# Four small edits to a TensorE-bound hybrid attention block: earlier mean squares, earlier activation sums, a tied order of the first splits, and another buffer ring for one tanh

## The chip, the cores and the metric

The kernel runs on one core of a Trainium2 chip. The metric is the device time of one execution in microseconds (us). Five engines work side by side, each through its own queue in order: TensorE (PE in the profile, with its weight loads as PEld), VectorE (DVE), ScalarE (ACT), GpSimd (POOL) and SyncE (SP), which only issues transfers here. ScalarE and GpSimd issue transfers too.

## The reference

One decoder block on x of 512 rows by 1024 columns, float32. Two attention branches of 8 heads of 64 read one normalised input:

```
h = rms_norm(x, norm_g)
proj = h @ w_in          # fq fk fv fz | mq mk mv mz | ga gb | fl
q, k = rms_norm per head (fq, fk); log_f = log_sigmoid(fl + b_f)
y_fox  = softmax(q k^T / 8 + cumsum(log_f) differences, causal) v * silu(fz)
q, k = partial_rope(rms_norm per head (mq, mk))
y_moba = block-sparse causal attention(q, k, mv) * silu(mz)
merged = sigmoid(ga + b0) * (y_fox @ w_fox) + sigmoid(gb + b1) * (y_moba @ w_moba)
out = x + merged @ w_out
```

With 512 rows and MoBA blocks of 256 all earlier blocks are selected, so that the second branch is plain causal attention in what it computes.

## The kernel before, in words

**Products in three parts.** Every product runs on operands that are split into a high part (rounded to the type that TensorE multiplies) and a low part (the rest): high × high, high × low and low × high are summed in PSUM. A split is one ScalarE copy for the high part and one VectorE subtraction for the low part. So each weight chunk that comes in (`wr`) becomes `wh` and `wl`, and each activation becomes a pair such as `Zh`/`Zl` or `Gh`/`Gl`.

**The start.** `first_loads` fetches the transposed x in 8 blocks (`XT`, tiles `xt`) and the first weight chunk in four pieces, by turns, on SyncE's queue. `first_split` (lines 148 to 160) splits the pieces of that chunk and, in the order of its argument `between`, the blocks of x (`split_x`, lines 120 to 126): `Zh`, `Zl`. For the first two pieces VectorE makes the high part too (line 155). `first_qk` multiplies the two first column groups, `fqa` and `fka`, from these unnormalised x (lines 382 to 384), four PSUM banks each, block after block of x; the factor of the row norm comes in later.

**The row norm.** `x_stats` (lines 221 to 232) loads x once more, not transposed, in 8 tiles, squares each on ScalarE with a running sum, and takes the power −1/2 on GpSimd: r. `norm_row` lays r out as a row with four TensorE transposes (bank `p_rbc`, line 240) and a ScalarE copy, `rbc`. `normalise` (lines 243 to 247) then multiplies the x blocks with it and splits them into `Gh` and `Gl`, which all later projections read; the first is `fva`.

**Attention.** Four groups of four heads (fox a, fox b, moba a, moba b) run one after another. In each, `Tr` transposes q and k, `Aa` makes logits in the two banks of "lg" (lines 555 and 556), subtracts the maximum on VectorE (`negm`, line 558) and takes exp on ScalarE (line 560), and `Bb` transposes the probabilities and multiplies with v (bank `pv`), after which ScalarE copies one half out (`ysh`, line 635) and VectorE adds the other. Between these steps the function `inter` puts units of other projections ("fill") by turns: in the first group 16 of them (`fqb`, `fkb`, `fvb`, `mqa`, four each), in the last `mzb` and the products with `w_fox` (`wf0` to `wf2`, banks `pf`). `unit_z` (lines 413 to 426) computes z·(1 + tanh(z/2)), twice the silu, straight from a PSUM bank of the ring "pj" (2 banks): tanh on ScalarE into a tile `sg`, then a VectorE operation into `zs` (line 425), which frees the bank. The factor 1/2 is put into the row sums of the softmax.

**Activation sums.** `make_sums(k)` (lines 257 to 277), for k from 0 to 3, makes four sums and differences of normalised x blocks on VectorE (line 265), splits them, and stores them to DRAM through ScalarE's queue (line 275). The "gates" stage reads them back for the `ga` and `gb` products, which run as a seven-product Strassen scheme.

**Who sets the order.** The program text only gives a priority: a planner goes through it with estimated times and writes each engine's queue, taking of what it holds ready the piece that stands first in the text. `tc.issue_after(ins)` ties the pieces of its block behind `ins` on that engine. Tiles come from rings by tag: "u" with 4 tiles of 128 × 512, "y" with 15, and in PSUM "pj" 2, "tp" 3, "lg" 2, "pv" 1. A tile can be had only when an earlier one of its ring has been released.

Of the kernel before, what the change touches and what calls it, by code (L numbers as in the profile page):

```python
# [7 lines left out]
F32 = mybir.dt.float32  # L8
F32R = mybir.dt.float32r
AF = mybir.ActivationFunctionType  # L10
OP = mybir.AluOpType
# [5 lines left out]
NT = S // P  # L17
KT = D // P
HD = 64
CW = 256  # L20
# [9 lines left out]
def fox_moba_kernel(ctx: ExitStack, tc, xT, x, w_in, w_fl, w_fox, w_moba, w_out, cst, rope, out):  # L30


    nc = tc.nc
    V, A, G, T = nc.vector, nc.scalar, nc.gpsimd, nc.tensor
# [14 lines left out]
    def t2(tag, bufs, name, shape=(P, 512), dt=F32):  # L49
        pool = stage["pool"] if tag in ("qs", "pt", "pc", "ys") else sb  # L50
        return pool.tile(list(shape), dt, name=name, tag=tag, bufs=bufs)
# [39 lines left out]
    def col(c, n=1):  # L91
        return cs[:, c:c + n]
# [13 lines left out]
    for i in range(WARM):  # L106
# [6 lines left out]
    G.memset(mask, 0.0)  # L113
    G.affine_select(mask[:, 384:512], mask[:, 384:512], pattern=[[-1, P]], compare_op=OP.is_ge,
                    fill=NEG, base=0, channel_multiplier=1)

    Gh = con.tile([P, KT, S], F32R, name="Gh")
    Gl = con.tile([P, KT, S], F32R, name="Gl")
# [2 lines left out]
    def split_x(*ks):  # L121
        for k in ks:
            xt = XT[k]
            zh, zl = Z[k] = [stage["pool"].tile([P, S], F32R, name=f"Z{hl}{k}") for hl in "hl"]
            A.activation(zh, xt, AF.Copy, scale=col(C_NG + k))
            V.scalar_tensor_tensor(zl, xt, col(C_NG + k), zh.bitcast(F32), op0=OP.mult, op1=OP.subtract)


    chunks = {}
# [18 lines left out]
    def first_split(hf, between):  # L148
        raw = RAW[hf]
        hi = sb.tile([P, 4, 264], F32R, name=f"wh_fqa{hf}", tag="wh", bufs=4)  # L150
        lo = sb.tile([P, 4, 264], F32R, name=f"wl_fqa{hf}", tag="wl", bufs=4)
        for q, xs in enumerate(between):
            k = slice(2 * q, 2 * q + 2) if hf else slice(max(q, 2 * q - 2), max(q + 1, 2 * q))
            if hf == 0 and q < 2:
                V.tensor_copy(hi[:, k, :CW], raw[:, k])
            else:
                A.activation(hi[:, k, :CW], raw[:, k], AF.Copy)
            V.tensor_tensor(out=lo[:, k, :CW], in0=raw[:, k], in1=hi[:, k, :CW].bitcast(F32), op=OP.subtract)
            split_x(*xs)
        chunks.setdefault("fqa", []).append((hi, lo))  # L160

# [59 lines left out]
    def x_stats():  # L221
        G.memset(mh, -0.5)
        for t in range(NT):
            for hf in range(2):
                xt = t2("y", 15, f"x{t}{hf}")
                nc.sync.dma_start(out=xt, in_=x[t * P:(t + 1) * P, hf * 512:(hf + 1) * 512])
                j = t2("u", 4, "junk")
                A.activation(j, xt, AF.Square, accum_out=ms2[:, t, hf:hf + 1])
        V.tensor_add(mm, ms2[:, :, 0], ms2[:, :, 1])
        V.tensor_scalar(mm, mm, 1.0 / D, EPS, op0=OP.mult, op1=OP.add)  # L230
        V.tensor_scalar(e2, mm, EPS, None, op0=OP.mult)
        G.tensor_tensor(out=r, in0=mm, in1=mh[:, :NT], op=OP.pow)
# [4 lines left out]
    def norm_row():  # L237
        p = pst("lg", 2, "p_rbc")
        for t in range(NT):
            T.transpose(p[:, t * P:(t + 1) * P], r[:, t:t + 1].to_broadcast([P, P]), ident)  # L240
        A.activation(rbc, p, AF.Copy)
# [132 lines left out]
    def first_qk(name, tags):  # L374
        banks = [pst(tg, n, f"{name}_{i}") for i, (tg, n) in enumerate(tags)]
        n = 264 if name == "fka" else CW
        for kk in range(KT):
            hi, lo = chunks[name][kk // 4]
            k = kk % 4
            for t in range(NT):  # L380
                st = slice(t * P, (t + 1) * P)
                T.matmul(banks[t][:, :n], Z[kk][0][:, st], hi[:, k, :n], start=(kk == 0), stop=False)
                T.matmul(banks[t][:, :n], Z[kk][0][:, st], lo[:, k, :n], start=False, stop=False)
                T.matmul(banks[t][:, :n], Z[kk][1][:, st], hi[:, k, :n], start=False, stop=(kk == KT - 1))
        return banks
# [27 lines left out]
    def unit_z(name, c):  # L413
        def go():
            p = (tp if name == "fzb" else pj)(f"pz_{name}{c}")
            tr_mm(p, name, c)
            z = t2("y", 15, f"zs_{name}{c}")
            s = t2("u", 4, "sg")
            if name[0] == "f":
                V.tensor_tensor(out=z, in0=p, in1=rbc, op=OP.mult)  # L420
                A.activation(s, z, AF.Tanh, scale=0.5)
                V.scalar_tensor_tensor(z, s, 1.0, z, op0=OP.add, op1=OP.mult)
            else:
                A.activation(s, p, AF.Tanh, scale=0.5)
                V.scalar_tensor_tensor(z, s, 1.0, p, op0=OP.add, op1=OP.mult)  # L425
            ZS[name[0], 2 * (name[2] == "b") + c] = z
        return go
# [586 lines left out]
                res.append(go)  # L1014
        return res

    def last_on(engine):
        return next(i for i in reversed(nc.cur_bb.bb.instructions) if i.engine == engine)

    def inter(a, b):  # L1020
        n, m = len(a), len(b)
        ia = ib = 0
# [9 lines left out]
        for u in filler(names):  # L1032
            u()

    first_split(0, ((0,), (1, 2), (3, 4)))
    first_split(1, ((5, 6), (7,)))
    nc.sync.dma_start(out=wfl, in_=w_fl)
    load_fl("fka", COLS["fka"], 0)
    load_fl("fka", COLS["fka"], 1)
    b1 = first_qk("fqa", (("pj", 2), ("pj", 2), ("lg", 2), ("lg", 2)))  # L1040
    b2 = first_qk("fka", (("tp", 3), ("tp", 3), ("tp", 3), ("pv", 1)))
    x_stats()
    for t in range(NT):
        evac_qk(b1[t], "fqa", t)
    for t in range(NT):
        evac_qk(b2[t], "fka", t)
    forget_exp()
    norm_row()
    pump(0)
    fz = filler(["fza", "fzb"])  # L1050
    for k, u in enumerate(fz):
# [14 lines left out]
    for n in range(4):  # L1066
        nxt = []

        def following(n=n, nxt=nxt):
            br, half, cq, ck = plan[n + 1][:4]  # L1070
            if n == 1:
                moba_begin()
            nxt.extend(attn_group(br, half, col(cq), col(ck)))
            nxt[0][0]()
        fill = filler(plan[n][4])
        if n == 0:
            for k in range(4):
                store = []

                at = 3 * k + 5  # L1080

                def with_sums(u=fill[at], k=k, store=store):
                    u()
                    with tc.issue_after(last_on(mybir.EngineType.DVE)):
                        store.append(make_sums(k))

                def with_store(u=fill[at + 1], store=store):
                    u()
                    store[0]()
                fill[at], fill[at + 1] = with_sums, with_store  # L1090
        inter(body + ([following] if n < 3 else []) + tail, fill)
        if n < 3:
            at = 2
            body, tail = nxt[1][:at] + gate + nxt[1][at:], nxt[2]
            gate = nxt[3]
# [10 lines left out]
    groups["WO"]()  # L1106
    prep, product, evac, sub, result = (groups[k] for k in ("prep", "product", "evac", "sub", "out"))

    def behind():
        return tc.issue_after(last_on(mybir.EngineType.DVE))  # L1110
    m1, m3 = filler(["wm1"]), filler(["wm3"])
    if True:
        m1[0]()
# [111 lines left out]
```

## Time and profile before

| | |
|---|---|
| median of 3 runs | 427.01 us (426.59 to 427.05) |
| the profiled execution's own time | 426.79 us |
| its span | 424.8 us |
| TensorE busy | 418.6 us, 99% |
| VectorE busy | 326.7 us, 77% |
| ScalarE busy | 269.3 us, 63% |
| GpSimd busy | 100.7 us, 24% |
| mean granted TensorE clock | 0.999 |

The span counts from the first to the last instruction of the program; some 2 us lie around it. In a row of a timeline stand the start and the length in us, engine, line, operation, out<-in by the program's names, the shape, and in brackets the idle time of the engine before it with what ended it. Rows of one tile give lengths in ns as least/median/most. A busy TensorE is not a TensorE at its peak, since matmuls overlap: there the distance from start to start is what counts.

### The profile page before, as it was taken

Reading aid. Unit: us, or ns where it says so; the run is one execution under the profiler, and the core shown is the slowest. Engines: PE = TensorE matmul, PEld = TensorE weight load, DVE = VectorE, ACT = ScalarE, POOL = GpSimd, SP = SyncE. Lnnn points to the kernel's source line nnn. Section 1 sums busy time; section 2 is a strip of 40 time slices with the busy share of each in tenths; the row PEclk is TensorE's granted clock in tenths of the full one; section 3 lists DMA queues with packets and bytes.
Section 4 is the critical chain, followed back from the end, with each engine's and each line's share of the span. In section 5 each row is a group of like instructions: output and inputs, shape, how many; then the busy total and the mean of one; then the engine's idle time right before and its main releaser. Section 6 shows DMA issues by size and latency. Waiting matters only on the chain.

```text
span 424.8 us, 7715 instructions
## 1 busy us (share of the span) xinstructions
PE 418.6 (99%) x2913; PEld 388.9 (92%) x2913; DVE 326.7 (77%) x570; ACT 269.3 (63%) x515; POOL 100.7 (24%) x120
## 2 busy tenths in 40 slices
PE   8999999999999999999999999999999999999996
PEld 7998899999999998899998878899999989988885
DVE  4669976769969878578576697767979598689893
ACT  4986426866857977567656687665756535686450
POOL 1049200225133950016650103140000000022330
PEclk9999999999999999999999999999999999999999
DMA  7981235225485423203124131663052603696484
GB/s 241 392 304 67 84 115 154 77 90 198 154 227 173 114 100 125 92 33 125 32 94 116 63 95 44 224 226 127 19 182 64 234 2 117 208 252 118 99 145 154
DMA packets 25621, 58.21 MB, mean 137 GB/s; under 512 B 3064, under 2 KB 7856, under 8 KB 25584
## 3 DMA queue, kind: packets, MB, share of 16 engines
q1 hardware_dynamic: 13392, 38.11, 26.6%
q10 hardware_dynamic: 8800, 11.21, 8.7%
q0 software_dynamic: 3392, 8.39, 8.6%
q8 instruction: 23, 0.38, 0.4%
q14 instruction: 14, 0.11, 0.1%
HBM read 48.11 MB, written 6.32 MB: 128 GB/s over the span
## 4 chain that ended last, share of the span: by engine, by line
PE 65%; DVE 1%; ACT 1%; issue 0%
PE pb_GB L753 3%; PE pb_GA L753 3%; PE pb_GA L750 3%; PE pb_GB L750 3%; PE pb_GB L752 3%; PE pb_GA L752 3%; PE po L941 3%; PE po L940 3%; PE po L939 3%; PE pf L679 2%; PE pv L611 2%; PE pm L681 2%; PE pf L681 2%; PE pf L680 2%; PE pv L610 2%; PE pm L680 2%
## 5 line engine op out<-in xcount | busy, mean ns | idle before, releaser
L560 ACT ACTIVATE p<-p,negm 128x128 f32<-128x128 f32 (+1 forms) x64 | 35.7, 559 | 20.8 <-DVE negm L558 18.4
L334 POOL TENSOR_TENSOR ff<-ss,mh 128x8 f32<-128x8 f32 x16 | 27.2, 1702 | 79.0 <-DVE ss L332 78.7
L558 DVE CUSTOM_DVE_ANT_0 p<-lg,mask 128x128 f32<-128x128 f32 (+1 forms) x64 | 30.5, 486 | 13.3 <-PE lg L556 13.1
L888 POOL DMA_DIRECT2D wr_o<-in_w_out_dram x4 | 4.9, 1295 | 95.4 <-ACT wr_o L887 95.4
L555 PE MATMUL lg<-KH,QS 128*128 128x128 f32 (+1 forms) x64 | 20.6, 333 | 0.2 <-DVE negm L558 0.2
L134 ACT ACTIVATE wh_GB<-wr_gb 128x1024 fp32r<-128x1024 f32 x14 | 14.6, 1059 | 9.5 <-PE pm L680 3.5
L136 DVE TENSOR_TENSOR wl_GA<-wr_ga,wh_GA 128x1024 fp32r<-128x1024 f32 x14 | 16.9, 1224 | 4.7 <-ACT wh_GA L134 3.9
L901 ACT ACTIVATE wh_o<-wr_o 128x1024 fp32r<-128x1024 f32 x14 | 14.8, 1057 | 8.3 <-PE pb_GB L752 2.8
L134 ACT ACTIVATE wh_GA<-wr_ga 128x1024 fp32r<-128x1024 f32 x14 | 14.6, 1059 | 8.3 <-issue 3.0
L902 DVE TENSOR_TENSOR wl_o<-wr_o,wh_o 128x1024 fp32r<-128x1024 f32 x14 | 17.0, 1222 | 3.7 <-ACT wh_o L901 3.4
L636 DVE TENSOR_TENSOR ypair<-pv,ysh 64x512 f32<-64x512 f32 x16 | 11.0, 688 | 11.2 <-ACT ysh L635 10.9
L136 DVE TENSOR_TENSOR wl_GB<-wr_gb,wh_GB 128x1024 fp32r<-128x1024 f32 x14 | 16.9, 1223 | 3.5 <-ACT wh_GB L134 3.5
L607 DVE TENSOR_TENSOR ptl<-p_a,pth 128x512 fp32r<-128x512 f32 x16 | 11.0, 686 | 6.8 <-ACT pth L606 6.7
L635 ACT ACTIVATE ysh<-pv 64x512 f32<-64x512 f32 x16 | 9.5, 593 | 7.8 <-POOL qn_mqa L336 2.5
L750 PE MATMUL pb_GA<-Gh,wh_GA 128*128 128x256 f32 x48 | 13.6, 282 | 0.0
L752 PE MATMUL pb_GA<-Gl,wh_GA 128*128 128x256 f32 x48 | 13.5, 281 | 0.0
L679 PE MATMUL pf<-yhf,wh_wf 128*128 128x512 f32 x32 | 12.8, 400 | 0.7 <-DVE zs_mzb L425 0.7
L753 PE MATMUL pb_GA<-Gh,wl_GA 128*128 128x256 f32 x48 | 13.5, 281 | 0.0
L753 PE MATMUL pb_GB<-Gh,wl_GB 128*128 128x256 f32 x48 | 13.5, 281 | 0.0
L752 PE MATMUL pb_GB<-Gl,wh_GB 128*128 128x256 f32 x48 | 13.4, 281 | 0.0
L750 PE MATMUL pb_GB<-Gh,wh_GB 128*128 128x256 f32 x48 | 13.3, 281 | 0.0
L529 DVE SCALAR_TENSOR_TENSOR QS<-p_qT,cs,QS 64x512 fp32r<-64x512 f32 x16 | 12.0, 750 | 1.6 <-ACT QS L528 1.1
(459 smaller groups left out, 1795.4 us busy)
## 6 DMA issues: line engine op xcount, KB each, us to landing
wr_ga<-in_w_in_dram SPq DMA_DIRECT2D x8, 512.0 KB
wr_gb<-in_w_in_dram SPq DMA_DIRECT2D x8, 512.0 KB
wr_o<-in_w_out_dram SPq DMA_DIRECT2D x8, 512.0 KB
xt<-in_xT_dram SPq DMA_DIRECT2D x8, 256.0 KB
x<-in_x_dram SPq DMA_DIRECT2D x8, 256.0 KB
KH<-KH ACTq DMA_DIRECT2D x16, 128.0 KB
s_dramh<-sum_sh ACTq DMA_DIRECT2D x8, 256.0 KB
s_draml<-sum_sl ACTq DMA_DIRECT2D x8, 256.0 KB
```

Source lines behind the costliest of these rows:

```text
L134: A.activation(hi[:, :, 0:n], src, AF.Copy)
L136: eng.tensor_tensor(out=lo[:, q, 0:n], in0=src[:, q], in1=hi[:, q, 0:n].bitcast(F32), op=OP.subtract)
L334: G.tensor_tensor(out=f2, in0=ss.rearrange("p t h -> p (t h)"), in1=mh, op=OP.pow)
L555: T.matmul(lg[:, :n], qs[:, qt], kh[:, :n], start=True, stop=False)
L558: V.tensor_tensor_reduce(pt, lg[:, :n], mask[:, 512 - n:512], -0.125, 3.0e38, op0=OP.add, op1=OP.min, accum_out=mkn[:, hh, i:i + 1])
L560: A.activation(pt, pt, AF.Exp, bias=mkn[:, hh, i:i + 1], scale=-1.0, accum_out=rs[:, hh, i:i + 1])
L679: T.matmul(p, hi[:, k, cc], yh, start=(k == 0), stop=False)
L680: T.matmul(p, hi[:, k, cc], yl, start=False, stop=False)
L750: T.matmul(o, hi[:, k, cc], lh, start=(n < 3 and c == 0 and k == 0), stop=False, skip_group_check=True)
L752: T.matmul(o, hi[:, k, cc], ll, start=False, stop=False, skip_group_check=True)
L753: T.matmul(o, lo[:, k, cc], lh, start=False, stop=(k == 3), skip_group_check=True)
L902: V.tensor_tensor(out=wide(lo), in0=wide(R[key, c]), in1=wide(hi).bitcast(F32), op=OP.subtract)
```

## The change

- Mean squares: the two tiles of the last quarter of x come from the ring "u" instead of "y"; ScalarE writes the squares over x itself instead of into a tile `junk`; and in the text the statistics, the evacuation of `fqa` and `norm_row` stand ahead of the products of `fka`.
- Activation sums: packet k is attached to fill unit 3k instead of 3k + 5, its stores to the unit after it.
- First splits: all their VectorE instructions are tied behind the last VectorE instruction of the text, so that VectorE takes them in the order of the text; and block 4 of x moves from the first half's last step to the second half's first one, with blocks 5, 6 and 7 following.
- The tanh of `mzb`: its tile `sg` comes from the ring "y" instead of "u".

The helpers `last_on` and `behind` move up in the file; what they do is unchanged.

```diff
+    def last_on(engine):
+        return next(i for i in reversed(nc.cur_bb.bb.instructions) if i.engine == engine)
+
+    def behind(engine=mybir.EngineType.DVE):
+        return tc.issue_after(last_on(engine))
...
             A.activation(zh, xt, AF.Copy, scale=col(C_NG + k))
-            V.scalar_tensor_tensor(zl, xt, col(C_NG + k), zh.bitcast(F32), op0=OP.mult, op1=OP.subtract)
+            with behind():
+                V.scalar_tensor_tensor(zl, xt, col(C_NG + k), zh.bitcast(F32), op0=OP.mult, op1=OP.subtract)
...
             if hf == 0 and q < 2:
-                V.tensor_copy(hi[:, k, :CW], raw[:, k])
+                with behind():
+                    V.tensor_copy(hi[:, k, :CW], raw[:, k])
             else:
                 A.activation(hi[:, k, :CW], raw[:, k], AF.Copy)
-            V.tensor_tensor(out=lo[:, k, :CW], in0=raw[:, k], in1=hi[:, k, :CW].bitcast(F32), op=OP.subtract)
+            with behind():
+                V.tensor_tensor(out=lo[:, k, :CW], in0=raw[:, k], in1=hi[:, k, :CW].bitcast(F32), op=OP.subtract)
             split_x(*xs)
...
-                xt = t2("y", 15, f"x{t}{hf}")
+                xt = t2("u", 4, f"x{t}{hf}") if t == NT - 1 else t2("y", 15, f"x{t}{hf}")
                 nc.sync.dma_start(out=xt, in_=x[t * P:(t + 1) * P, hf * 512:(hf + 1) * 512])
-                j = t2("u", 4, "junk")
-                A.activation(j, xt, AF.Square, accum_out=ms2[:, t, hf:hf + 1])
+                A.activation(xt, xt, AF.Square, accum_out=ms2[:, t, hf:hf + 1])
...
-            s = t2("u", 4, "sg")
+            s = t2("y", 15, "sg") if name == "mzb" else t2("u", 4, "sg")
...
-    first_split(0, ((0,), (1, 2), (3, 4)))
-    first_split(1, ((5, 6), (7,)))
+    first_split(0, ((0,), (1, 2), (3,)))
+    first_split(1, ((4, 5), (6, 7)))
...
     b1 = first_qk("fqa", (("pj", 2), ("pj", 2), ("lg", 2), ("lg", 2)))
-    b2 = first_qk("fka", (("tp", 3), ("tp", 3), ("tp", 3), ("pv", 1)))
     x_stats()
     for t in range(NT):
         evac_qk(b1[t], "fqa", t)
+    norm_row()
+    b2 = first_qk("fka", (("tp", 3), ("tp", 3), ("tp", 3), ("pv", 1)))
     for t in range(NT):
         evac_qk(b2[t], "fka", t)
     forget_exp()
-    norm_row()
...
-                at = 3 * k + 5
+                at = 3 * k
```

More of the change, by code (lines that the diff above doesn't have):

```diff
@@ L1015, in filler @@
         return res
-    def last_on(engine):
-        return next(i for i in reversed(nc.cur_bb.bb.instructions) if i.engine == engine)
     def inter(a, b):
@@ L1107, in fox_moba_kernel @@
     prep, product, evac, sub, result = (groups[k] for k in ("prep", "product", "evac", "sub", "out"))
-    def behind():
-        return tc.issue_after(last_on(mybir.EngineType.DVE))
     m1, m3 = filler(["wm1"]), filler(["wm3"])
```

## The prediction

> **What bounds the kernel now.** I read the engine totals of the page first, then TensorE's list of waits, then the timelines around each place where TensorE stood still, and last the load of VectorE by stretch.
>
> ```profile
> PE 418.6 (99%) x2913; PEld 388.9 (92%) x2913; DVE 326.7 (77%) x570; ACT 269.3 (63%) x515; POOL 100.7 (24%) x120
> ```
>
> TensorE (PE) is busy for 99% of the span of 424.8 us. The diff neither adds nor removes a matmul, so it can only win back time in which TensorE stood still, or add such time.
>
> ```profile
> PE pf L679 <- DVE zs_mzb L425: 0.7, 1, 0.7
> PE lg L555 <- DVE negm L558: 0.2, 1, 0.2
> ```
> ```profile
> 421.30:424.90 3.60, 0.00 (x0) 0.00 (x0) 0.42 (x1) 0.00 (x0) 0.00 (x0) 0.85 0.26 88
> ```
>
> After the start, the list of waits names just two: 0.7 us before the first product with `w_fox` and 0.2 us before a block of logits. The last row (busy time by engine from 421.30 on) is the tail, where TensorE has finished; the diff does not touch it. What can be gained is therefore these two stalls and what is lost in the first 14 us. Everything else that the diff makes earlier is earlier on engines that TensorE was not waiting for.
>
> **The tanh of the last z.** These are the four places that matter: TensorE ends the first half of `mzb`; ScalarE (ACT) and VectorE (DVE) stand idle; ScalarE runs the two tanhs; TensorE waits.
>
> ```profile
> 232.69 0.40 PE L407 MATMUL pz_mzb<-Gh,wl_mzb 128*128 128x512 f32 x1
> ```
> ```profile
> 235.47 0.60 ACT L606 ACTIVATE pth<-p_a 128x512 fp32r<-128x512 f32 x1 [2.84 <-PE p_cc L600]
> ...
> 242.91 0.59 ACT L635 ACTIVATE ysh<-pv 64x512 f32<-64x512 f32 x1
> 243.52 1.09 ACT L424 ACTIVATE sg<-pz_mzb 128x512 f32<-128x512 f32 x2
> ```
> ```profile
> 236.10 0.69 DVE L607 TENSOR_TENSOR ptl<-p_a,pth 128x512 fp32r<-128x512 f32 x1 [4.17 <-ACT pth L606]
> ```
> ```profile
> 244.28 0.40 PE L556 MATMUL lg<-KL,QS 128*128 128x512 f32 x1
> 245.39 0.50 PE L679 MATMUL pf<-yhf,wh_wf 128*128 128x512 f32 x1 [0.71 <-DVE zs_mzb L425]
> 245.72 0.40 PE L680 MATMUL pf<-ylf,wh_wf 128*128 128x512 f32 x1
> ```
>
> The input of the first tanh is complete at 232.69 + 0.40 = 233.09, yet the tanh starts at 243.52, 10.4 us later, though ScalarE idled 2.84 us up to 235.47 and VectorE 4.17 us up to 236.10. It starts directly behind `ysh` (242.91 + 0.59 = 243.50). Both write tiles of the ring "u" (4 tiles), and in the program's text the `ysh` of the preceding head stands ahead of this tanh: I read the order as the ring handing out its tiles in order of the text, so that the tanh queues behind a `ysh` that it has no need of. Until `zs_mzb` has read `pz_mzb`, its bank of the ring "pj" (2 banks) is not free for `pf`.
>
> With the tanh's tile in the ring "y" (15 tiles) that order is gone. By the text, the tiles of "y" alive there are 8 of `yhf`/`ylf`, 2 of `zs_mza`, 2 of the first `yhm`/`ylm` and `zs_mzb` itself: 13, and the tanh makes 14, so there is room. I expect the first tanh between 233.1 and 235.5 and its bank free some 8 us sooner. Price of the stall: 245.39 − 244.28 = 1.11 from start to start, where a product of this width takes 0.23 (below, 53.16 − 52.93), so 0.88; and the restart, 245.72 − 245.39 = 0.33 instead of 0.23, so 0.10. **Term: −0.98 us**, from 0 (ScalarE's order stays) to −0.98. Late next is the bank of the second half, whose tanh also moves forward.
>
> **Activation sums five units sooner.** The four packets (lines 265 to 275) move by five of the 16 units of the first attention stage, some 18 us by where they lie now. Nothing is added; VectorE, ScalarE and the stores of ScalarE's queue all move along.
>
> ```profile
> L265 DVE TENSOR_TENSOR sum_sf<-xt,sum_sf x4: 415/447/1525, 97.9 to 132.1; 128x256 f32<-128x256 f32 x4
> L269 DVE TENSOR_TENSOR sum_sl<-sum_sf,sum_sh x8: 676/680/693, 101.9 to 134.3; 128x512 fp32r<-128x512 f32 x8
> ```
> ```profile
> L275 ACTq DMA_DIRECT2D s_dramh<-sum_sh x8: 361/370/482, 100.0 to 133.4; - x8
> ```
> ```profile
> 62.00:82.00 20.00, 20.00 (x170) 19.91 (x169) 13.15 (x32) 13.56 (x29) 2.68 (x2) 1.00 0.34 96
> 82.00:98.00 16.00, 16.00 (x131) 15.64 (x130) 11.99 (x29) 12.06 (x31) 4.95 (x4) 1.00 0.31 102
> 98.00:138.00 40.00, 40.00 (x330) 39.49 (x330) 36.08 (x71) 27.32 (x58) 12.66 (x12) 1.00 0.64 195
> ```
>
> A packet holds four additions (about 0.42 each, the least of the row being 0.415) and two differences (0.68 each), so 4 × 0.42 + 2 × 0.68 = 3.0 us of VectorE; its four stores hold ScalarE's queue for 0.37 each, 1.5 us. The third number after the window is VectorE's busy time: 13.15 of 20, 11.99 of 16, then 36.08 of 40. The packets go from the fullest stretch into two with 6.9 and 4.0 us free, which hold the first two of them. Their stores only have to land before the "gates" stage, far behind.
>
> What TensorE gets is the second stall, which comes 6 us after the last packet's last rows (134.3):
>
> ```profile
> 141.13 0.28 PE L307 MATMUL pj_mka<-wl_mka,Gh 128*128 128x256 f32 x1
> 141.62 0.50 PE L555 MATMUL lg<-KH,QS 128*128 128x512 f32 x1 [0.20 <-DVE negm L558]
> ```
> ```profile
> 140.16 1.04 POOL L336 TENSOR_TENSOR qn_mqa<-qn_mqa,ff 128x512 f32<-128x512 f32 x1
> ```
> ```profile
> 140.21 1.02 DVE L332 TENSOR_SCALAR ss<-ss 128x8 f32<-128x8 f32 x1
> ```
>
> Price: 141.62 − 141.13 = 0.49 instead of 0.12, so 0.37, plus a restart of 0.10 as above: 0.47. VectorE came late with `negm`, at the end of a stretch it worked through at 90%, and the last straw was one tiny instruction of 8 numbers that took 1.02 us beside GpSimd's (POOL's) multiplication. With 3 us taken out of that stretch VectorE should arrive there early enough. **Term: −0.47**, from 0 to −0.47; I take it whole because the work removed is six times the lateness.
>
> That last pair of rows speaks against the move too: the packets hold 24 instructions of VectorE with two inputs in SBUF, and one of their additions took 1.525 us beside a median of 0.447 and a least of 0.415, so they can be caught as well. The Trainium skill, SBUF — State Buffer (section "Who interferes with whom"), has a rule for it: VectorE and GpSimd share one port pair; an instruction of VectorE with two SBUF inputs contends with one of GpSimd that reads SBUF, and a `tensor_scalar` may contend as well; whoever comes second waits for the whole instruction. The trace agrees at 140.21 (held until GpSimd's end at 141.20). By that rule packets that land beside GpSimd's multiplications at 79 and 88 us are held up there: that is rival (c), at 427.7, where the rows above alone give 425.4.
>
> **Order of the first splits tied.** VectorE now follows the text: the low half of weight blocks 2 and 3 (line 158) comes behind `Zl` of x blocks 1 and 2. Before, it ran ahead of the latter.
>
> ```profile
> 8.37 0.69 DVE L158 TENSOR_TENSOR wl_fqa<-wr_fqa,wh_fqa 128x512 fp32r<-128x512 f32 x1 [0.24 <-ACT wh_fqa L157]
> 9.14 0.75 DVE L126 SCALAR_TENSOR_TENSOR Zl<-xt,cs,Zh 128x512 fp32r<-128x512 f32 x1
> ```
> ```profile
> 9.46 0.28 PE L382 MATMUL fqa<-wh_fqa,Zh 128*128 128x256 f32 x1
> 9.58 0.28 PE L383 MATMUL fqa<-wl_fqa,Zh 128*128 128x256 f32 x1
> 9.94 0.39 PE L384 MATMUL fqa<-wh_fqa,Zl 128*128 128x256 f32 x1
> ...
> 12.68 0.28 PE L384 MATMUL fqa<-wh_fqa,Zl 128*128 128x256 f32 x1
> 13.06 0.39 PE L382 MATMUL fqa<-wh_fqa,Zh 128*128 128x256 f32 x1
> ```
> ```profile
> 12.30 1.32 ACT L125 ACTIVATE Zh<-xt,cs 128x512 fp32r<-128x512 f32 x2
> ```
>
> A product of 256 columns takes 0.12 from start to start. TensorE loses 0.24 at 9.58 (`Zl`) and 0.26 at 12.68 (`Zh` of block 4, ready about half way through ScalarE's pair that starts at 12.30, so 12.96). With the tie, `Zl` still runs 9.14 to 9.89, and the low half then takes 0.69, to 10.6 instead of 9.06. TensorE can do block 2's four high products at 9.46 to 9.93 and then waits to 10.6; eight products and a restart bring it to 11.7, block 3's twelve to 13.1. There it used to stand until 13.06 anyway. So one wait takes the place of another. **Term: +0.1**, from −0.1 to +0.4 (the latter if only one high product can go ahead: 10.6 + 11 × 0.12 + 0.1 = 12.0, and 13.45 after block 3). Moving x block 4 into the second half changes the text's place of `Zh`, whose data had already been waiting on ScalarE's pair of weight copies; it is inside these bounds.
>
> **Mean squares sooner.** The last x tile was the 16th of a ring of 15, so its load went out last:
>
> ```profile
> 19.29 1.03 SPq L349 DMA_DIRECT2D rp<-in_rope_dram  x1
> 20.41 0.38 SPq L226 DMA_DIRECT2D x<-in_x_dram  x1
> ```
> ```profile
> 29.06 1.05 POOL L232 TENSOR_TENSOR r<-mm,mh 128x4 f32<-128x4 f32 x1
> ```
> ```profile
> 34.91 0.60 PE L240 MATMUL p_rbc<-ident,r 128*128 128x128 f32 x4
> ```
> ```profile
> 50.63 1.29 DVE L247 TENSOR_TENSOR Gl<-xt,Gh 128x512 fp32r<-128x512 f32 x2
> ```
> ```profile
> 52.93 0.39 PE L407 MATMUL pz_fzb<-Zh,wl_fzb 128*128 128x512 f32 x1
> 53.16 0.28 PE L306 MATMUL pj_fva<-wh_fva,Gh 128*128 128x256 f32 x1
> ```
>
> In the ring "u" it can go ahead of the four weight loads and the rope table, at about 16.5, so r comes 4 to 5 us sooner, near 25.5. The eight squares cost the same; only their output goes back into x. The four weight loads land one x tile later, under a microsecond, with several in hand. The normalised `Gl` then ends near 47 instead of 51.92; `fva` needs it at 53.16 and was not waiting: slack grows from 1.2 us to 6. **Term: 0.**
>
> **Sum.** The profiled execution took 426.79 us, 0.2 below the median of the three (427.01; they spread over 0.46). 426.79 − 0.98 − 0.47 + 0.1 = 425.4; I forecast 425.5. About 0.2% (0.85 us) is what a measurement of this kernel can tell from no change. The likeliest case has its own range of 424.8 to 426.1: below, if the 0.5 us of losses in the first 14 us go as well; above, if one small new stall like that of 141 us appears, since all engines' orders are planned anew.
>
> **Rivals.**
> (a) *Only one stall goes.* The tanh alone: 426.79 − 0.98 + 0.1 = 425.9, chance 0.15. The sums alone, with the bank of `pf` still late because ScalarE's planned order keeps the tanh behind `ysh`: 426.4, chance 0.08. For the latter speaks that ScalarE's queue is in order; against it the 2.84 us it stood idle.
> (b) *Nothing is won*: the stalls only move to other places. 426.9, chance 0.10.
> (c) *Slower: the packets meet GpSimd's multiplications at 79 to 98 us.* VectorE then brings `negm` late, TensorE has two logit banks and stands.
>
> ```profile
> 79.10 1.04 POOL L336 TENSOR_TENSOR qn_fqb<-qn_fqb,ff 128x512 f32<-128x512 f32 x1
> ...
> 88.54 1.04 POOL L336 TENSOR_TENSOR qn_fqb<-qn_fqb,ff 128x512 f32<-128x512 f32 x1
> ```
>
> Each of the four packets may lose up to 1.04 us on top of its 3.0. Passed on to TensorE in full, with a 0.10 restart, that is 4 × 1.14 = 4.6; half of it is 2.3, giving 425.4 + 2.3 = 427.7. It is slower by over 0.2% once 2.3 us are passed on, two whole hits. For it: the planner of the order evidently did not foresee the 1.02 us at 140.21. Against: TensorE has projection units to fill with, and in 62 to 138 us it never waited. Chance 0.16. By the skill's port rule this is what happens wherever the two overlap.
> (d) *The transposes of r stand too early in TensorE's queue.* `norm_row` is now ahead of `fka`, whose products start here:
>
> ```profile
> 18.80 0.29 PE L382 MATMUL fka<-wh_fka,Zh 128*128 128x264 f32 x1
> ```
>
> If the transposes came first, TensorE would stand from 18.8 to about 25.5: 6.7 us, 432.1. Against: they were placed in the middle of `fza`, 4.8 us after r was ready (30.11), so the order follows estimated readiness, on the late side. Chance 0.06.
>
> **How the numbers follow.** The forecast has the remaining 0.45. Faster by over 0.2% (below 426.1): 0.45 + 0.15 = 0.60. Same: 0.08 + 0.10 = 0.18. Slower: 0.16 + 0.06 = 0.22. The range reaches from 424.6 (both stalls and the start's losses gone, within 0.2) to 427.9 (c); it leaves out (d) and some of (c).
>
> **What would show it.** Right: the tanh `sg<-pz_mzb` starts within 3 us of its product, the row `pf <- zs_mzb` is gone from TensorE's waits, the sums' rows start near 77 us and the last ends before 120, the wait on `negm` near 141 is gone, `fva` still does not wait, and block 2's products wait for `wl_fqa` at about 10. Wrong: new rows of TensorE waiting for `negm`, or for r ahead of `p_rbc`; additions of over 1 us beside `L336`; or a tanh still right behind `ysh`.

## The result, and the profile after

The changed kernel takes 425.43 us (median of 7 runs, 425.22 to 425.72) against 426.77 us (426.35 to 427.05) for the kernel before on the same chip: a ratio of 0.9967, 95% interval 0.9957 to 0.9977, or 1.3 us less. Measured a second time on another chip, beside three of the experiments below, it came to 0.9978 (0.9966 to 0.9989). Its profiled execution took 425.43 us with a span of 423.4; before, 426.79 and 424.8.

The engine totals of the page of the changed kernel: the number of instructions is the same on every engine, TensorE (PE) is busy 0.9 us less.

```profile
PE 417.7 (99%) x2913; PEld 388.9 (92%) x2913; DVE 326.8 (77%) x570; ACT 269.5 (64%) x515; POOL 106.3 (25%) x120
```

TensorE's list of waits in the changed kernel, whole (total us, times, longest):

```profile
PE warm_ps L107 <- DVE fg_pre L480: 1.5, 1, 1.5
PE fqa L392 <- DVE wl_fqa L168: 0.5, 1, 0.5
```

The two rows that the prediction read, `pf <- zs_mzb` and `lg <- negm`, are gone. What remains is the warm-up, as before, and one wait at the start.

The timeline around the tanhs of `mzb` (start, length, engine, line; in brackets the idle time before it and what ended it), ScalarE (ACT) and then TensorE:

```profile
232.60 0.60 ACT L433 ACTIVATE sg<-pz_mzb 128x512 f32<-128x512 f32 x1 [0.49 <-PE pz_mzb L416]
...
241.05 0.58 ACT L433 ACTIVATE sg<-pz_mzb 128x512 f32<-128x512 f32 x1
...
242.03 0.59 ACT L644 ACTIVATE ysh<-pv 64x512 f32<-64x512 f32 x1
...
241.84 0.40 PE L688 MATMUL pf<-yhf,wh_wf 128*128 128x512 f32 x1
242.08 0.40 PE L689 MATMUL pf<-ylf,wh_wf 128*128 128x512 f32 x1
```

The first tanh now waits only for its product, and both stand ahead of `ysh` (242.03). The first `pf` product carries no wait, and the second follows 0.24 us later, without a restart.

The activation sums, least/median/most in ns, first and last start in us (one line of the four kinds of addition, and the differences), and the busy time of the engines in the second and third of the prediction's stretches (the first number behind the window is its length; then come the busy times of PE, PEld and VectorE, the last being the one read here):

```profile
L274 DVE TENSOR_TENSOR sum_sf<-xt,sum_sf x4: 372/420/424, 71.3 to 113.4; 128x256 f32<-128x256 f32 x4
L278 DVE TENSOR_TENSOR sum_sl<-sum_sf,sum_sh x8: 672/684/693, 72.6 to 117.3; 128x512 fp32r<-128x512 f32 x8
```
```profile
82.00:98.00 16.00, 16.00 (x130) 15.62 (x130) 14.97 (x37) 13.49 (x34) 2.68 (x2) 1.00 0.52 163
98.00:138.00 40.00, 40.00 (x326) 39.36 (x325) 32.96 (x70) 29.05 (x64) 18.27 (x16) 1.00 0.49 155
```

VectorE's load from 98 to 138 us fell from 36.08 to 32.96 of 40, and the middle stretch filled up to 14.97 of 16. The kind of addition that took up to 1.525 us before now takes at most 0.424, and the other three kinds at most 0.426: none of the moved additions was held up beside GpSimd (POOL).

The start, TensorE and VectorE (DVE); the products of 256 columns follow one another in 0.12 us where nothing holds them:

```profile
9.30 0.64 PE L391 MATMUL fqa<-wh_fqa,Zh 128*128 128x256 f32 x4
10.47 0.39 PE L392 MATMUL fqa<-wl_fqa,Zh 128*128 128x256 f32 x1 [0.54 <-DVE wl_fqa L168]
...
12.84 0.28 PE L393 MATMUL fqa<-wh_fqa,Zl 128*128 128x256 f32 x1
12.96 0.28 PE L391 MATMUL fqa<-wh_fqa,Zh 128*128 128x256 f32 x1
```
```profile
9.06 0.75 DVE L133 SCALAR_TENSOR_TENSOR Zl<-xt,cs,Zh 128x512 fp32r<-128x512 f32 x1 [0.56 <-ACT Zh L131]
9.73 0.68 DVE L168 TENSOR_TENSOR wl_fqa<-wr_fqa,wh_fqa 128x512 fp32r<-128x512 f32 x1
```

The low half is ready at 9.73 + 0.68 = 10.41; four high products go ahead of it, then TensorE stands. Block 4 starts at 12.96, where it stood until 13.06 before: as the prediction had it, one wait has taken the place of another.

The mean squares: r, its four transposes and the last of the normalised low parts:

```profile
24.79 1.04 POOL L241 TENSOR_TENSOR r<-mm,mh 128x4 f32<-128x4 f32 x1 [22.44 <-DVE mm L239]
27.85 0.60 PE L249 MATMUL p_rbc<-ident,r 128*128 128x128 f32 x4
```
```profile
43.49 1.29 DVE L256 TENSOR_TENSOR Gl<-xt,Gh 128x512 fp32r<-128x512 f32 x2
```

r starts 4.3 us sooner (24.79 instead of 29.06) and the last `Gl` ends at 44.78 instead of 51.92.

### The profile page after: what moved, and what is told of

Read it like the earlier page. It is cut to its first block, busy times and chain, and to the rows that moved or that the text cites. A ratio compares the mean times of both kernels' runs of the same rounds, so it can differ in the third digit from the quotient of the medians.

```text
span 423.4 us, 7713 instructions
## 1 busy us (share of the span) xinstructions
PE 417.7 (99%) x2913; PEld 388.9 (92%) x2913; DVE 326.8 (77%) x570; ACT 269.5 (64%) x515; POOL 106.3 (25%) x120
## 4 chain that ended last, share of the span: by engine, by line
PE 97%; DMA 1%; SPq 0%; DVE 0%; issue 0%; ACT 0%
PE pb_GB L762 3%; PE pb_GA L762 3%; PE pb_GB L759 3%; PE pb_GA L759 3%; PE pb_GB L761 3%; PE pb_GA L761 3%; PE po L950 3%; PE po L949 3%; PE po L948 3%; PE lg L565 2%; PE pv L620 2%; PE pv L619 2%; PE lg L564 2%; PE pf L690 2%; PE pf L689 2%; PE pm L690 2%
## 5 line engine op out<-in xcount | busy, mean ns | idle before, releaser
L343 POOL TENSOR_TENSOR ff<-ss,mh 128x8 f32<-128x8 f32 x16 | 32.0, 2005 | 71.0 <-DVE ss L341 63.2
L337 DVE TENSOR_REDUCE ss<-sq 128x8 f32<-128x512 f32 x16 | 10.9, 679 | 4.6 <-ACT sq L336 4.5
L542 DVE SCALAR_TENSOR_TENSOR KL<-p_kT,cs,KH 64x512 fp32r<-64x512 f32 x16 | 12.0, 749 | 1.3 <-ACT KH L540 0.8
L537 ACT ACTIVATE QS<-p_qT,cs 64x512 fp32r<-64x512 f32 x16 | 10.9, 680 | 3.3 <-DVE QS L538 2.2
```

The lines of the kernel that those rows point to most:

```text
L343: G.tensor_tensor(out=f2, in0=ss.rearrange("p t h -> p (t h)"), in1=mh, op=OP.pow)
```

## The experiments

Theory: the gain is the two stalls, each taken away by its own edit (the tanh's ring, the sums' place), while the mean squares and the first splits are worth nothing. Each edit was first run alone on the kernel before. The four share one chip and 35 runs of the kernel before (median 426.64).

**The tanh alone** (e1_tanh):

```diff
-            s = t2("u", 4, "sg")
+            s = t2("y", 15, "sg") if name == "mzb" else t2("u", 4, "sg")
```

> The kernel before with one edit: the tile of the last z's tanh comes from the ring "y". Theory (the tanh queued behind ysh in the ring "u", and pf waited for its bank): the wait of pf on zs_mzb is gone and nothing else moves, 0.98 us less, ratio about 0.9977; the wait on negm near 141 us stays at 0.2 us. Rival (the stall goes only together with the earlier sums, as ScalarE is too full): the wait of pf stays above 0.4 us and the ratio above 0.999.

Measured 425.83 us, 0.9985 (0.9971 to 0.9998): 0.64 us less. In the list of TensorE's waits `pf <- zs_mzb` is gone and others have come; the profiled execution, 427.48 us, was the longest of its twelve.

```profile
PE pv L610 <- DVE ypair L636: 0.9, 1, 0.9
PE fqa L384 <- DVE Zl L126: 0.6, 1, 0.6
PE lg L555 <- DVE negm L558: 0.5, 2, 0.3
```

The waits on `negm` are two here, at 132.39 and 143.22; they cost 0.32 and 0.48 from start to start beyond the regular distance. So the stall that the prediction saw once has a second one of its kind, which the profiled execution of before happened not to show. Of the other kernels below that leave the sums and the mean squares alone, e5_ysh and e6_u5 show both as well (0.30 and 0.47, 0.31 and 0.48), e3_split only the later one (0.32). The earlier of the two comes behind an addition of a packet that was itself held up beside a multiplication of GpSimd (e1_tanh, VectorE and GpSimd; other additions take about 0.41):

```profile
130.87 1.26 DVE L265 TENSOR_TENSOR sum_sf<-sum_sf,xt 128x256 f32<-128x256 f32 x1
```
```profile
130.37 1.48 POOL L661 TENSOR_TENSOR rinv_bc<-zs_fza,rinv_bc 128x512 f32<-128x512 f32 x1 [3.83 <-DMA rinv_bc<-r_dram]
```

**The sums alone** (e2_sums):

```diff
-                at = 3 * k + 5
+                at = 3 * k
```

> The kernel before with one edit: the packets of activation sums sit at fill unit 3k instead of 3k + 5. Theory (VectorE came late with negm near 141 us because of the packets before it): the wait on negm near 141 us is gone, 0.47 us less, ratio about 0.9989; the wait of pf on zs_mzb stays at 0.7 us. Rival (VectorE was held by GpSimd's multiplication, whatever went before): a wait on negm of 0.2 us or more stays somewhere from 130 to 150 us and the ratio is 0.9995 or more. Second rival (packets beside GpSimd's multiplications at 79 to 98 us): new waits on negm there, ratio above 1.001.

Measured 425.87 us, 0.9979 (0.9969 to 0.9989): 0.9 us less (0.5 to 1.3), about twice the term of 0.47, which lies at the edge of the interval. No wait on `negm` is left anywhere. The wait of `pf` is still there, but of 0.26 us instead of the 0.71 of the kernel before:

```profile
243.71 0.40 PE L556 MATMUL lg<-KL,QS 128*128 128x512 f32 x1
244.37 0.51 PE L679 MATMUL pf<-yhf,wh_wf 128*128 128x512 f32 x1 [0.26 <-DVE zs_mzb L425]
244.71 0.40 PE L680 MATMUL pf<-ylf,wh_wf 128*128 128x512 f32 x1
```

From start to start that is 0.66 − 0.23 = 0.43, and 0.34 − 0.23 = 0.11 for the restart: 0.54 in all.

**The first splits alone**, tie and order (e3_split): of the diff only `behind()` and the two calls of `first_split`.

> The kernel before with the first splits tied and block 4 of x moved to the second half. Theory of the prediction: the wait of block 2 on wl_fqa takes the place of the two waits on Zl and Zh in the first 14 us, +0.1 us, ratio 1.000 (0.9998 to 1.001). The trace of the changed kernel suggests 0.2 us less for all of the first 20 us, ratio 0.9995. Rival (the tie is what wins the time): ratio under 0.998.

Measured 426.77 us, 1.0002 (0.999 to 1.0013). The wait is the one foreseen, and both stalls of the kernel before stand (their lines are shifted by ten):

```profile
PE fqa L393 <- DVE wl_fqa L168: 0.7, 1, 0.7
PE pf L689 <- DVE zs_mzb L435: 0.3, 1, 0.3
PE lg L565 <- DVE negm L568: 0.2, 1, 0.2
```

**The mean squares alone** (e4_stats): of the diff only the last x tiles in "u", the squares in place, and statistics and `norm_row` ahead of `fka`.

> The kernel before with the mean squares' edits alone (last quarter of x in the ring "u", squares in place, statistics and norm_row ahead of the products of fka in the text). Theory: no effect on TensorE, which was not waiting: ratio 1.000 within 0.0007; r some 4 to 5 us sooner. Rival 1 (the transposes of r stand too early in TensorE's queue): a new wait of TensorE ahead of p_rbc, ratio above 1.002. Rival 2 (the new order of VectorE's work in 30 to 60 us removes the wait on negm near 141 us): that wait is gone without the sums having moved, ratio about 0.999.

Measured 427.03 us, 1.0018 (1.0002 to 1.0035): slower, if barely. A wait has come that no kernel above has:

```profile
PE lg L564 <- DMA KH<-KH: 2.4, 1, 2.4
```

`KH` is the key table of the next group; a transfer of 128 KB copies part of it from SBUF to SBUF. TensorE stands 2.4 us for it before the first logits of moba a. So the term of 0 for this edit holds only beside the others, and the question became what makes the table late.

The next four share another chip and 32 runs of the kernel before (median 426.83). Two of them ask why the tanh was late. Theory: the ring gives its tiles out in the order of the text, so the tanh stands behind a `ysh`. Rival: "u" is just too small.

**The `ysh` out of the ring instead of the tanh** (e5_ysh), on the kernel before:

```diff
-                sh = t2("u", 4, "ysh")
+                sh = t2("y", 15, "ysh") if br + half == "ma" and h > 1 else t2("u", 4, "ysh")
```

> The kernel before, with the tanh left in the ring "u" and instead the tile ysh of the third and fourth heads of the first MoBA group taken from the ring "y". Theory (the ring gives out its tiles in the order of the text, and these two ysh stand ahead of the tanh): the first tanh of mzb runs soon after its product, as in the changed kernel, the wait of pf on zs_mzb is gone, about 1 us less, ratio 0.9977. Rival (the tanh itself has to leave a full ring, or ScalarE's planned order holds it back): the tanh still starts behind ysh near 243 us, ratio 1.000.

**One tile more in "u"**, one fewer in "y" (e6_u5), on the kernel before: every `"u", 4` becomes `"u", 5`, every `"y", 15` becomes `"y", 14`.

> The kernel before with the ring "u" at 5 tiles instead of 4, and "y" at 14 instead of 15 for the room. Theory (order of the text): a fifth tile changes nothing, both tanhs start directly behind ysh near 243 us and pf waits about 0.7 us; ratio within 0.001 of 1. Rival (the ring was full): the first tanh starts before 237 us and the wait of pf is gone, ratio 0.9977.

Measured 426.22 us, 0.9988 (0.9973 to 1.0003), and 426.39 us, 0.9991 (0.9981 to 1.0001). The times do not separate them; ScalarE's order does. With the `ysh` in "y":

```profile
234.18 0.60 ACT L424 ACTIVATE sg<-pz_mzb 128x512 f32<-128x512 f32 x1 [0.49 <-PE pz_mzb L407]
238.41 0.60 ACT L635 ACTIVATE ysh<-pv 64x512 f32<-64x512 f32 x1 [0.95 <-issue]
...
243.45 0.57 ACT L424 ACTIVATE sg<-pz_mzb 128x512 f32<-128x512 f32 x1
```
```profile
244.72 1.28 DVE L425 SCALAR_TENSOR_TENSOR zs_mzb<-sg,pz_mzb 128x512 f32<-128x512 f32 x2
```

With five tiles in "u":

```profile
242.87 0.59 ACT L635 ACTIVATE ysh<-pv 64x512 f32<-64x512 f32 x1
243.49 1.09 ACT L424 ACTIVATE sg<-pz_mzb 128x512 f32<-128x512 f32 x2
```

Whichever of the two leaves the ring, the first tanh starts right behind its product; with a tile more it still comes directly behind `ysh`. So the order is what holds it, and room for one tile more does not help; a still larger ring was not tried. In e5_ysh a wait of 0.2 us for `zs_mzb` stays all the same: VectorE's operations that read both tanhs and free both banks start only at 244.72, although the first tanh had ended at 234.78. In the changed kernel the first of them starts at 233.23. The tanh's place alone was thus not enough there; why VectorE took its part so late is not shown.

**The changed kernel without the tanh's edit** (e7_no_tanh):

> The changed kernel with the tanh put back into the ring "u". Theory (effects add): the wait of pf on zs_mzb is back at about 0.7 us and the kernel takes about 1 us more than the changed one, 426.4, ratio to before 0.999. Rival (with the sums earlier, ScalarE and VectorE have room there anyway): no such wait, ratio 0.997.

Measured 425.84 us, 0.9974 (0.9964 to 0.9984). The wait of `pf` is back with 0.26 us, a stall of 0.43 + 0.10 = 0.53 with the restart, as in e2_sums:

```profile
243.51 0.40 PE L565 MATMUL lg<-KL,QS 128*128 128x512 f32 x1
244.17 0.49 PE L688 MATMUL pf<-yhf,wh_wf 128*128 128x512 f32 x1 [0.26 <-DVE zs_mzb L434]
244.50 0.39 PE L689 MATMUL pf<-ylf,wh_wf 128*128 128x512 f32 x1
```

In time its interval overlaps both measurements of the changed kernel, so the 0.53 rests on the profile; that the tanh's edit shortens the kernel beside the others is not shown by the times.

**The changed kernel without the sums' edit** (e8_no_sums):

> The changed kernel with the packets of activation sums put back to unit 3k + 5. Theory (effects add): a wait on negm of about 0.2 us near 140 us is back, the kernel takes 0.4 to 0.5 us more than the changed one, 425.9, ratio to before 0.998. Rival (that wait was a chance meeting of VectorE with GpSimd, and any new order ends it): no such wait, ratio 0.997.

Measured 426.89 us, 1.0002 (0.999 to 1.0013): without this one line the whole gain is gone. The wait is not the one on `negm` but again the key table's:

```profile
113.81 0.37 ACTq L284 DMA_DIRECT2D s_draml<-sum_sl  x1
114.31 0.40 ACTq L284 DMA_DIRECT2D s_dramh<-sum_sh  x1
114.80 0.49 ACTq L541 DMA_DIRECT2D KH<-KH  x1
...
120.90 0.33 PE L564 MATMUL lg<-KH,QS 128*128 128x128 f32 x1 [1.12 <-DMA KH<-KH]
```

The same rows of the changed kernel:

```profile
114.33 0.48 ACTq L541 DMA_DIRECT2D KH<-KH  x1
114.94 0.51 ACTq L284 DMA_DIRECT2D s_dramh<-sum_sh  x1
...
118.98 0.22 PE L564 MATMUL lg<-KH,QS 128*128 128x128 f32 x1
```

And the first logits of this group in the kernel before:

```profile
126.85 0.22 PE L555 MATMUL lg<-KH,QS 128*128 128x128 f32 x1
```

There the table, issued at 114.96, had 12 us to arrive. The sums' edit and the mean squares' edit each make the planner take these logits 5 to 8 us sooner (119.15 in e2_sums, 122.07 in e4_stats, wait included), and so take that slack away. Where the sums are late and the mean squares early, two of the sums' stores stand ahead of the table in ScalarE's queue; in the changed kernel they come behind it. In e2_sums one stands ahead, and TensorE does not wait.

The last four share a third chip and 32 runs of the kernel before (median 426.56); **the changed kernel again** (e9_after) is the measure for the rest.

> The changed kernel again, as the measure for the three beside it on this chip. Both theories expect 0.9967 of the kernel before, 425.4 us. In its chain the largest wait of TensorE is the one for the low half of blocks 2 and 3 of wf near 9.9 us, 0.5 to 0.7 us.

Measured 425.56 us (425.1 to 426.95), 0.9978 (0.9966 to 0.9989); the wait for the low half is 0.6 us.

**The stores of the sums on SyncE's queue** (e12_no_sums_sp), with the sums late as in e8_no_sums:

```diff
-                A.dma_start(out=d, in_=t)
+                nc.sync.dma_start(out=d, in_=t)
...
-                at = 3 * k
+                at = 3 * k + 5
```

> The changed kernel with the activation sums five units later, as before the change (the order that made TensorE wait 1.1 us for the gathered key table near 119 us), and the stores of the sums issued on SyncE's queue instead of ScalarE's. Theory (the table's transfer stands behind those stores in ScalarE's queue): the wait near 119 us is gone, and the time is about 1.2 us below that order's 426.9, that is 0.997 to 0.998 of the kernel before. Rival (the table is late because the sixteen transfer engines are shared, whichever queue the stores are in, or since its own inputs are late): the wait of 1 us or more stays, ratio 1.000.

Measured 426.21 us, 0.9989 (0.9972 to 1.0005), between the two expectations and by its interval compatible with both. The profile tells more:

```profile
114.65 0.49 ACTq L541 DMA_DIRECT2D KH<-KH  x1
...
119.98 0.33 PE L564 MATMUL lg<-KH,QS 128*128 128x128 f32 x1 [0.43 <-DMA s_draml<-sum_sl]
```

From issue to product the table takes 5.33 us here, 6.10 in e8_no_sums (114.80 to 120.90), and at most 4.65 in the changed kernel, where TensorE did not wait. (The row names a store of the sums as the last to end the wait, which no product reads; the weight load in front of it waited for `KH`.) So more than half of the wait went (1.12 us became 0.43), and the rest stayed. The edit changed more than the queue, though: the two stores that were issued ahead of the table in e8_no_sums (113.81 and 114.31) went out behind it here, at 115.20 and 116.01. So the run shows the table without them; it does not show what they would cost in the other queue at the same time. The trace also has a record of each packet of a transfer. The first packet of the table, beside what was issued shortly before (us; a store counts as ahead where its packets were still to come when the table was issued):

```
kernel          load wr_mza  stores ahead in      KH      KH's first  after KH's  after the
                issued       ScalarE's queue      issued  packet      issue       load's issue
before          114.68       none                 114.96  117.39      2.43        2.71
after           113.48       none                 114.33  116.02      1.69        2.54
e9_after        113.88       none                 114.72  116.50      1.78        2.62
e12_no_sums_sp  114.59       none                 114.65  117.38      2.73        2.79
e2_sums         113.51       114.29               114.86  116.91      2.05        3.40
e8_no_sums      114.81       113.81, 114.31       114.80  118.40      3.60        3.59
e4_stats        115.00       113.87, 114.37       114.86  118.28      3.42        3.28
```

In the four profiles without a store ahead, and in the seven others of that kind (2.55 to 2.73), the table's first packet follows the issue of the 512 KB weight load on SyncE's queue by 2.5 to 2.8 us, whenever the table itself was issued: the two queues are not independent. The packets say more. Each of these transfers ends in 16 packets of 4 bytes, and in all eleven profiles the table's first packet starts 3 to 6 ns after the first of the load's 16 (117.391 after 117.385 us in before). So the table began when the load's first part was through, or so the times read. A store ahead adds to that, partly by delaying the load itself: the load's own first packet came 1.50 us after its issue in e8_no_sums and 1.47 in e4_stats, against 0.96 in before. The Trainium skill, DMA: Bandwidth & Descriptors, has a rule that bears on this: its section "Issuing engines are not separate DMA queues" has transfers of all engines end up on the same 16 DMA engines, and "Queues, rings and completion order" that SyncE's and ScalarE's queues have no DMA engine or descriptor generator of their own. The trace agrees: the start of the table on one queue follows the load on the other to within 6 ns. Moving the weight load alone was not tried, so that its share is read from the packets, not shown by an experiment. Open is also e4_stats, where the first packet is no later than in e8_no_sums but the product came 1.2 us later.

**The low half ahead of the second `Zl`** (e10_lowfirst), on the changed kernel:

```diff
-    first_split(0, ((0,), (1, 2), (3,)))
+    first_split(0, ((0,), (1,), (2, 3)))
```

> The changed kernel with the low half of blocks 2 and 3 ahead of the second split of x on VectorE, in the same tie. Theory (VectorE's order sets the start): the low half takes 0.68 us and is ready some 0.75 us sooner, the wait for it (0.5 us and 0.1 us of restart) is gone; what is late next is the split of x that block 4 waits for, ready near 12.5 us, so 0.3 to 0.5 us less than the changed kernel, 0.9955 to 0.996 of the kernel before. Rival (the arrival of x and of the weights sets the start): block 4 starts near 12.96 us as it does in the changed kernel, and the time is the changed kernel's within 0.1 us.

**The same with ScalarE tied in the second half** (e11_acttie): `Zh` of blocks 4 to 7 and the two high halves of the second weight copies under `behind(mybir.EngineType.Activation)`.

> The run before, and on ScalarE the high halves of the second weight copies and of the three blocks of x beside them tied in the order written (copy 4 and 5, x block 4, x block 5, copy 6 and 7, x blocks 6 and 7). Theory (ScalarE's order is what the split of block 4 waits for): the high half of x block 4 starts one weight copy sooner, and the time is another 0.2 to 0.4 us less. Rival (the landing of x block 4, near 11.4 to 11.9 us, bounds it): no difference from the run before within 0.1 us.

Measured 425.37 us (0.9972, 0.996 to 0.9983) and 425.23 us (0.9972, 0.996 to 0.9983), 0.2 and 0.3 below the changed kernel on the same chip, with intervals that overlap its own. The profile of e10_lowfirst shows the wait for the low half replaced by one of 0.2 us:

```profile
PE fqa L393 <- DVE Zl L133: 0.2, 1, 0.2
```

That of e11_acttie has a wait of the same length, and the span is 423.1 us (423.2 for e10_lowfirst, 423.8 for e9_after). The foreseen 0.3 to 0.5 us of the first can be seen locally: from the first product of block 2 of x to that of block 3, TensorE takes 1.89 us in e10_lowfirst and 1.96 in e11_acttie, against 2.23 and 2.44 in the two profiles of the changed kernel. But the rival's sign is there too: block 2 began later in e10_lowfirst (9.57 against 9.30 in the first profile of the changed kernel), and block 4 starts at 12.89, where it started at 12.96. The further 0.2 to 0.4 of the second cannot be told from nothing. Both are the fastest of all that ran by their medians; that they beat the changed kernel is not shown.

## Why the prediction was right, and where it was not

Forecast 425.5 us, range 424.6 to 427.9; measured 425.43, and 425.56 the second time. Faster was the likeliest sign, with 0.60. The span fell by 1.4 us, and the two stalls that went were priced at 0.98 + 0.47 = 1.45. But single terms were off, and two of the errors cancel; that the sum came within 0.1 us is in part luck. The start plays in as well: the last product of `fqa` began at 18.68 in before and at 18.48 and 18.99 in the two profiles of the changed kernel; from there to the end of TensorE's work these two are 1.26 and 1.38 us shorter than before.

- **The tanh (−0.98): mechanism right, size wrong.** The order was that of the ring's text (e1_tanh, e5_ysh against e6_u5), and the tanh now starts right at its product. But −0.98 was the price in one execution. In five other kernels whose tanh still stands behind `ysh` (e2_sums, e3_split, e4_stats, e6_u5, e7_no_tanh) the wait is 0.26 and the stall 0.53 to 0.54; in time the edit alone gave 0.64 (0.1 to 1.2). The difference of 0.45 can be read from the rows, though no run tested it: VectorE was late. In before the logits of 128 columns were complete at 241.33 + 0.28 = 241.61, and VectorE took them up at 242.07, 0.46 later; in e3_split it took them up 0.04 after their end (241.68 + 0.27 = 241.95). From there to the operation on `zs_mzb` (244.65 and 244.53) it is 2.58 us in before and 2.54 in e3_split. What made VectorE late was its subtraction for `w_fox`, which started only 0.95 us ahead of the logits' end and took 1.48 us beside a multiplication of GpSimd, 0.25 more than the 1.23 of its next one.

These are the rows of the kernel before, TensorE, VectorE and GpSimd:

```profile
241.33 0.28 PE L556 MATMUL lg<-KL,QS 128*128 128x128 f32 x1
```
```profile
240.66 1.48 DVE L136 TENSOR_TENSOR wl_wf<-wr_wf,wh_wf 128x1024 fp32r<-128x1024 f32 x1 [0.18 <-ACT wh_wf L134]
242.07 0.28 DVE L558 CUSTOM_DVE_ANT_0 p<-lg,mask 128x128 f32<-128x128 f32 x1
...
242.32 1.23 DVE L136 TENSOR_TENSOR wl_wf<-wr_wf,wh_wf 128x1024 fp32r<-128x1024 f32 x1
```
```profile
239.76 1.30 POOL L661 TENSOR_TENSOR rinv_bc<-zs_mza,rinv_bc 128x512 f32<-128x512 f32 x1 [18.54 <-DMA rinv_bc<-r_dram]
```

And of e3_split, TensorE and VectorE:

```profile
241.68 0.27 PE L566 MATMUL lg<-KL,QS 128*128 128x128 f32 x1
```
```profile
241.99 0.29 DVE L568 CUSTOM_DVE_ANT_0 p<-lg,mask 128x128 f32<-128x128 f32 x1 [0.88 <-PE lg L566]
```

- **The sums (−0.47): mechanism right, size too small.** The wait on `negm` went with them, in e2_sums too. But the profiled execution of before showed one of two such waits; e1_tanh, e5_ysh and e6_u5 have both, 0.77 to 0.80 together without restarts, and the edit alone gave 0.9 us (0.5 to 1.3). The packets moved by more than the 18 us assumed: the first one's additions now start at 67.9 instead of 95.6, not near 77, and only the last end (117.3 + 0.69 = 118.0, before 120) came as written.
- **The first splits (+0.1): right in the steps, the size too small to tell.** The low half was ready at 10.41 (forecast 10.6), and block 2 waited for it from 9.94 to 10.47. The wait for `Zh` of block 4 was absorbed in the changed kernel, but not in e3_split: there `Zh` ended at 12.94 and block 4 began at 12.99, 0.23 us behind the regular distance. In time e3_split gave 1.0002 (0.999 to 1.0013), half a microsecond to either side.
- **The mean squares (0): right in the sum, wrong alone.** r came 4.3 us sooner, its transposes stood at 27.85 without a wait, and `fva` did not wait. The prediction looked at what the edit makes ready sooner and missed what the planner then does sooner: the first logits of the third group moved from 126.85 to 119, up to a transfer that had had 12 us to arrive. Alone, the edit costs 0.8 us (0.1 to 1.5). With late sums, as in e8_no_sums, the wait for that transfer eats what the other edits win. So the edits do not add up: the sums' edit is worth 0.9 us alone and, by the ratios of e8_no_sums and e9_after, about 1.0 beside the mean squares (1.5 by the first measurement; these are ratios from different chips), for a different reason each time.
- **Rival (a)**, one stall only: excluded by the list of waits. **Rival (b)**, the stalls move on: excluded by the same list.
- **Rival (c)**, packets beside GpSimd's multiplications at 79 and 88 us: it did not happen. GpSimd's multiplications for `qn_fqb` now run at 78.56 and 87.56, the sums' additions at 67.9 to 71.8, at 86.4 to 87.1 and from 88.7 on; none took over 0.43 us. Whether two would hold each other up there was therefore not tested. In their old place they were held up: an addition took 1.26 us in e1_tanh, ahead of a late `negm`. The rival's mechanism was thus part of what the kernel before lost.
- **Rival (d)**, transposes too early: the transposes did move forward, to 27.85, two us behind r (24.79 + 1.04 = 25.83), and TensorE was not held up by them.
- The mechanism that was slower, a transfer brought onto the path by work planned sooner, was in none of the rivals.

## What to carry to other kernels

Price a stall from several executions, or from several programs that share it, before the sum rests on it: here one profile showed one stall at nearly twice the size that five others had, and hid another that three others had. Where a planner writes the queues, an edit that makes something ready sooner also makes its users start sooner; look at every transfer that they read, and at what stands ahead of it, in its own queue and in the other ones. And where a tile's ring makes an instruction late, look at the order in which the text asks for tiles, not only at their number.

## What the runs showed of the hardware that was not expected

- A transfer of 128 KB within SBUF, on ScalarE's queue, sent its first packet 1.7 to 3.6 us after its issue. The spread followed what stood before it: 1.7 where the weight load on the other queue was 0.85 us older, 2.7 where it was issued within 0.1 us, 3.4 to 3.6 where two stores of 256 KB also stood ahead in its own queue. Without such a store it started 3 to 6 ns after the first of the 16 small packets that end the load on the other queue, in eleven profiles of eleven.
- One program gave stalls of different size from one execution to the next: the wait for the low half at the start was 0.54 us in one profile of the changed kernel and 0.65 in the other, and the second also had two waits of 0.3 us for `Zh`, which the first lacked, with spans of 423.4 and 423.8 us.
